# The q and z projections of a decoder layer as seven half-size block products instead of eight, with the head norm of q moved into the attention

## The chip, the cores and the metric

The kernel runs on one core of a Trainium2 chip. The metric is the device time of one execution in microseconds; lower is better. TensorE (PE) multiplies matrices, VectorE (DVE), ScalarE (ACT) and GpSimd (POOL) do the elementwise work, and SyncE (SP) issues every DMA transfer of this kernel from one queue.

## The reference, cut to what matters

Two layers over 2048 tokens of 1024 features, in float32: a gated MLP (layer A), then attention (layer B).

```python
h  = rms_norm(x, norm_g) * (1 + scale) + shift        # layer B; keys and values use an h of their own
qz = h @ w_in                                         # [2048, 1024] @ [1024, 4096]
q  = qz[..., :3072].reshape(2048, 24, 128)            # three groups of eight heads
z  = qz[..., 3072:]
q  = rms_norm(q, q_norm_g) * (128 ** -0.5)            # the head norm, per token and head
# for each group (dilations 1, 4, 16), a band of 128 keys back:
sc = q @ k.T - slope * dilation * distance
p  = exp(sc - max(sc)); l = sum(p); o = p @ v / l
y  = combined(o) * silu(z)
out = x + gate * (y @ w_out)
```

## The kernel before, in words

A TensorE operand here is a pair (hi, lo) whose sum is the float32 number, each part in a shorter format. One product of a k-tile therefore takes three matmuls, hi by hi, hi by lo and lo by hi (`mm3`, lines 241 to 244). Weights are split on the chip, each time they are loaded: ScalarE writes hi and VectorE, or every fourth time GpSimd, writes lo (`split`, lines 219 to 225).

The tokens are worked in four quarters of 512 (four token tiles of 128). In each quarter `layer_A` computes v, u, z and the output product of layer A, and `proj_B` then computes keys and values (`kv_block`, three blocks of 512 columns), q (`q_block`, six blocks) and z of layer B (`z_block`, two blocks). All of these blocks but u and z of layer A go through `dense`: eight k-tiles of weights, 512 columns each, meet two token tiles at a time, so a block is 8 x 4 x 3 = 96 matmuls of 128x512. The weights of a block are loaded 512 KB at a time by `wunits` (line 231) into two buffers (`rp`) and split into nine (`wp`). At the end of `layer_A` the new residual tile is normalised (line 511), transposed on TensorE (line 311), and made into the operands `hk` (for keys and values) and `hb` (for q and z) by `norm_T`.

The result of a q block is normalised per head at once (`head_norm_store`): a square on ScalarE (522), a reduce on VectorE (524), a power on GpSimd (213, 214), a multiplication on VectorE (527), and a store to DRAM (566). Attention later loads it from there in blocks of 128 queries and one key-value head (`attend`), in four stages that run one unit apart: transposes of keys and queries, scores with maximum and exponentials (681 to 685), transposes of the probabilities, and weighted values. VectorE adds the distance times the slope, a constant of the program, to the scores (681).

Attention and the other side work are generators, the fillers. After each k-step of a product, `tick` lets some of their steps be issued; `rate` says how many. The attention of groups 0 and 1 runs beside layer A of the next quarter; group 2 needs all tokens and runs inside the q blocks of quarter 3, at a rate of 5.8 steps a tick; the rest runs in `finish`, which also combines the groups and does the output product. The program is recorded in this order, and a scheduler then orders each engine's instructions and assigns the buffers of the pools before the program is built; on the chip every engine works its own list in order.

Of the kernel before, what the change touches and what calls it, by code (L numbers as in the profile page):

```python
# [18 lines left out]
P = 128  # L19
# [15 lines left out]
def trunk(ctx, tc, out, x, c, a_ada_w, a_ada_b, a_norm_g, a_w_in, a_sgu_g, a_w_spatial,  # L35
# [15 lines left out]
    ep = ctx.enter_context(tc.tile_pool(name="ep", bufs=4))  # L51
    bp = ctx.enter_context(tc.tile_pool(name="bp", bufs=2))
    sp = ctx.enter_context(tc.tile_pool(name="sp", bufs=4))
    ap_ = ctx.enter_context(tc.tile_pool(name="ap", bufs=2))
# [5 lines left out]
    qd = [dp.tile([S, D], F32, name=f"qd{g}") for g in range(3)]  # L60
# [3 lines left out]
    gd = dp.tile([2, D], F32, name="gd")  # L64

    fillers = []

    def fill(n):
        """run n steps of the waiting side work, taking turns"""
# [28 lines left out]
    # ---------------------------------------------------------------- constants  # L98
# [7 lines left out]
    def columns(rows, nm):  # L106
        """vectors (multiples of 128 long) as columns of one tile, with the column of each"""
# [19 lines left out]
    def late_constants():  # L127
# [11 lines left out]
    # distance table for [query i, key j of prev | own]: i - j + 128, BIG outside the band  # L139
    dist = cp.tile([P, 256], F32, name="dist")  # L140
    nc.gpsimd.iota(dist, pattern=[[-1, 256]], base=P, channel_multiplier=1,
                   allow_small_or_imprecise_dtypes=True)
    nc.gpsimd.affine_select(dist, dist, pattern=[[-1, 256]], compare_op=ALU.is_ge,
                            fill=BIG, base=P, channel_multiplier=1)
    nc.gpsimd.affine_select(dist, dist, pattern=[[1, 256]], compare_op=ALU.is_ge,
                            fill=BIG, base=0, channel_multiplier=-1)
# [21 lines left out]
    def column_sums(acc, nm):  # L168
        """sums over the partitions of 512 columns, as four feature-major columns"""
# [17 lines left out]
    def ada_affine(dst, w, bo, go, nm):  # L187
        """dst: (A, B) with h = A * x / rms(x) + B, feature-major columns"""
# [21 lines left out]
    # ---------------------------------------------------------------- helpers  # L210
# [8 lines left out]
    def split(hi, lo, src, pool=False):  # L219
        """src = hi + lo exactly, both in 12 significant bits"""  # L220
# [6 lines left out]
    def wunits(w, k0, n0, nm, nk=KT, ordered=False):  # L227
        us = []
        for kk in range(0, nk, 2):
            raw = rp.tile([P, 2, 512], F32, tag="raw", name=f"raw_{nm}{kk}")  # L230
            ld = nc.sync.dma_start(
                raw, w[(k0 + kk) * P:(k0 + kk + 2) * P, n0:n0 + 512].rearrange("(k p) n -> p k n", p=P))
            if ordered:
                tc.keep_in_program_order(ld)
            for j in range(2):
# [687 lines left out]
```

## Time and profile before

| what | value |
|---|---|
| timed runs before | 3148.74, 3144.09, 3141.40 us; median 3144.09 |
| span of the profiled execution | 3137.5 us |
| median of the timed runs less that span | 6.6 us |
| TensorE busy | 3053.7 us, 97% of the span |
| VectorE, ScalarE, GpSimd busy | 51%, 45%, 32% |
| DMA, mean over the span | 148 GB/s, 463.20 MB |
| granted TensorE clock, mean | 0.991 |

The profile is of one execution. Its own time outside the profiler is not listed; the three timed runs lie 3.9 to 11.2 us above its span, and the span is what the rows add up to. A busy time is the union of the instructions' durations, so overlapping instructions count once. In a row of a group, the number after x is the count, then come the busy time in us, the mean duration of one in ns, and the idle time of the engine just before these instructions with what ended it.

### The profile page before, as it was taken

The numbers are of one execution on the slowest core, as the hardware profiler recorded it, in microseconds if no ns is written. First come the engines' busy times: TensorE is split into PE (matmuls) and PEld (weight loads), VectorE is DVE, ScalarE is ACT, GpSimd is POOL, SyncE is SP. The second block draws the span as 40 slices with busy tenths as digits, with TensorE's granted clock in tenths as the row PEclk, the third lists the DMA queues.
The fourth block names the chain that finished last, engine by engine and source line by source line (L and its number), as shares of the span: only waits on it lengthen the run. The fifth ranks groups of instructions, "written<-read, shape, count | busy, mean of one in ns | idle before, by whom it ended". The sixth has DMA issues, their size and how long they took to land.

```text
span 3137.5 us, 42797 instructions
## 1 busy us (share of the span) xinstructions
PE 3053.7 (97%) x15264; PEld 2562.8 (82%) x15264; DVE 1599.4 (51%) x2808; ACT 1427.5 (45%) x3017; POOL 999.6 (32%) x1080
## 2 busy tenths in 40 slices
PE   6999999999999999999999999999999999999999
PEld 4788878888888878888888888888888778877887
DVE  6785343443544344445654444446554445548853
ACT  4323343346555243356454343465453436566431
POOL 4212233331223133334344233433353231132312
PEclk9999999999999999999999999999999999999999
DMA  6765244443433354443333344433333355567733
GB/s 231 232 205 162 94 147 148 145 158 105 131 108 108 111 158 141 155 149 110 111 105 105 131 146 153 154 125 125 101 100 109 118 174 176 178 209 264 256 131 135
DMA packets 294488, 463.20 MB, mean 148 GB/s; under 512 B 28058, under 2 KB 127612, under 8 KB 294276
## 3 DMA queue, kind: packets, MB, share of 16 engines
q1 hardware_dynamic: 294276, 460.47, 44.9%
q8 instruction: 121, 1.98, 0.3%
q14 instruction: 91, 0.75, 0.1%
HBM read 371.91 MB, written 88.48 MB: 147 GB/s over the span
## 4 chain that ended last, share of the span: by engine, by line
PE 81%; DVE 7%; DMA 5%; issue 3%; POOL 2%; ACT 2%; SPq 1%; POOLq 0%; DVEq 0%; ACTq 0%
PE pd_q L242 5%; PE pd_q L244 5%; PE pd_q L243 5%; PE pd_z L279 4%; PE pd_z L281 4%; PE pd_z L280 4%; PE pd_u L279 3%; PE pd_u L281 3%; PE pd_u L280 3%; PE po L732 3%; PE pd_o L244 3%; PE pd_o L242 3%; PE pd_o L243 3%; PE pd_v L244 3%; PE pd_v L242 3%; PE pd_v L243 3%
## 5 line engine op out<-in xcount | busy, mean ns | idle before, releaser
L242 PE MATMUL pd_q<-w_q,hbh 128*128 128x512 f32 x768 | 305.1, 397 | 0.0
L244 PE MATMUL pd_q<-w_q,hbl 128*128 128x512 f32 x768 | 299.8, 390 | 0.0
L243 PE MATMUL pd_q<-w_q,hbh 128*128 128x512 f32 x768 | 299.4, 390 | 0.0
L685 ACT ACTIVATE pr<-pr,stat 128x256 f32<-128x256 f32 (+1 forms) x384 | 172.7, 451 | 100.0 <-DVE stat L683 99.5
L242 PE MATMUL pd_v<-w_v,hAh 128*128 128x512 f32 x512 | 208.0, 406 | 1.3 <-ACT hAh L322 1.3
L279 PE MATMUL pd_u<-hAh,w_u 128*128 128x512 f32 x512 | 208.5, 407 | 0.0
L279 PE MATMUL pd_z<-hAh,w_z 128*128 128x512 f32 x512 | 204.5, 399 | 0.0
L244 PE MATMUL pd_v<-w_v,hAl 128*128 128x512 f32 x512 | 202.3, 395 | 0.0
L243 PE MATMUL pd_v<-w_v,hAh 128*128 128x512 f32 x512 | 201.9, 394 | 0.0
L281 PE MATMUL pd_u<-hAh,w_u 128*128 128x512 f32 x512 | 200.1, 391 | 0.0
L281 PE MATMUL pd_z<-hAh,w_z 128*128 128x512 f32 x512 | 199.9, 390 | 0.0
L280 PE MATMUL pd_u<-hAl,w_u 128*128 128x512 f32 x512 | 199.8, 390 | 0.0
L242 PE MATMUL pd_o<-w_o,yh 128*128 128x512 f32 x512 | 199.8, 390 | 0.0
L243 PE MATMUL pd_o<-w_o,yh 128*128 128x512 f32 x512 | 199.8, 390 | 0.0
L280 PE MATMUL pd_z<-hAl,w_z 128*128 128x512 f32 x512 | 199.7, 390 | 0.0
L244 PE MATMUL pd_o<-w_o,yl 128*128 128x512 f32 x512 | 199.4, 389 | 0.0
L221 ACT ACTIVATE w_q<-raw_q 128x512 fp32r<-128x512 f32 x192 | 116.2, 628 | 182.9 <-DMA raw_q<-in_b_w_in_dram 122.6
L221 ACT ACTIVATE w_o<-raw_o 128x512 fp32r<-128x512 f32 x128 | 77.9, 628 | 215.0 <-PE pd_o L244 120.5
L244 PEld LDWEIGHTS pd_q<-w_q,hbl 128*128 128x128 f32 x768 | 144.2, 188 | 30.7
L681 DVE SCALAR_TENSOR_TENSOR pr<-dist,ps 128x256 f32<-128x256 f32 (+1 forms) x384 | 118.7, 356 | 98.2 <-PE ps L671 54.5
L242 PEld LDWEIGHTS pd_q<-w_q,hbh 128*128 128x128 f32 x768 | 144.6, 188 | 27.7
L243 PEld LDWEIGHTS pd_q<-w_q,hbh 128*128 128x128 f32 x768 | 144.5, 188 | 27.6
(314 smaller groups left out, 7750.5 us busy)
## 6 DMA issues: line engine op xcount, KB each, us to landing
raw_q<-in_b_w_in_dram SPq DMA_DIRECT2D x96, 512.0 KB, 3.7
raw_v<-in_a_w_in_dram SPq DMA_DIRECT2D x64, 512.0 KB, 3.7
raw_u<-in_a_w_in_dram SPq DMA_DIRECT2D x64, 512.0 KB, 3.9
raw_z<-in_a_w_in_dram SPq DMA_DIRECT2D x64, 512.0 KB, 3.6
raw_o<-in_a_w_out_dram SPq DMA_DIRECT2D x64, 512.0 KB, 3.6
raw_kv<-in_w_kv_dram SPq DMA_DIRECT2D x48, 512.0 KB, 3.8
qd<-hs_q SPq DMA_DIRECT2D x96, 256.0 KB, 2.1
qt<-qd SPq DMA_DIRECT2D x96, 256.0 KB, 2.7
```

What stands on the lines that cost most here:

```text
L221: nc.scalar.activation(hi, src, AF.Copy)
L242: nc.tensor.matmul(pt, lh, u[:, 0, :], start=first, stop=False)
L243: nc.tensor.matmul(pt, lh, u[:, 1, :], start=False, stop=False)
L244: nc.tensor.matmul(pt, ll, u[:, 0, :], start=False, stop=last)
L279: nc.tensor.matmul(pts[i], wh, hh[:, k, :], start=k == 0, stop=False)
L280: nc.tensor.matmul(pts[i], wh, hl[:, k, :], start=False, stop=False)
L281: nc.tensor.matmul(pts[i], wl, hh[:, k, :], start=False, stop=k == KT - 1)
L681: nc.vector.scalar_tensor_tensor(pr[:, i, :], dist[:, 256 - w:256], slope * DIL[g], psc[:, i, :], ALU.mult, ALU.subtract)
L685: nc.scalar.activation(pr[:, i, :], pr[:, i, :], AF.Exp, bias=mneg[:, i:i + 1], scale=-1.0, accum_out=lsum[:, i:i + 1])
L732: nc.tensor.matmul(po[:, h * P:(h + 1) * P], u["pT"][h // hp][:, h % hp, j, :], u["kv"][:, j, kh, 1, :], start=j == 0, stop=j == nk - 1)
```

## The change

q and z of layer B are computed in four blocks of 1024 columns (three groups of q, and z). Each block multiplies [512 tokens x 1024] by [1024 x 1024] as a 2 x 2 arrangement of half-size blocks, by the scheme of Strassen in Winograd's form: seven products of [256 x 512] by [512 x 512] instead of eight, with sums of blocks before and after. In detail:

- The sums of weight blocks (four per block of columns) are computed once, during quarter 0, by a new filler, `combine_weights`, and kept in DRAM (`wt`): t1 and t3 are differences of neighbouring blocks, t2 and t4 differences taken from those.
- The sums of token blocks are made at the end of `layer_A` by `norm_T2`, which takes the place of `norm_T` there: seven operands in place of one `hb`, in four buffers of `big` instead of two.
- `dense_s` runs the seven products, 168 matmuls in all, into two pairs of PSUM tiles in turn, and adds the results on VectorE in new tiles (`st`, pool `tp`).
- The q rows are stored unnormalised, with eight more columns per row: the four head factors, and the slopes divided by them. Attention copies these eight columns (GpSimd), adds the distance times the slope over the factor, takes the maximum, multiplies it by the factor, and lets the exponential scale by the factor.
- Weights are loaded 256 KB at a time into six buffers of half the size, and split into eight instead of nine. The pool of the elementwise tiles (`ep`) has six instead of four. The output weights of `finish` are loaded through the pool `wp`.
- The order in `proj_B` becomes kv 2, kv 1, q 2, kv 0, q 1, q 0, z. The rates change: 1.7 instead of 1.5 in quarter 0 (which has the weight sums as well), 0.7 instead of 1.3 for the next quarter's input, 7.0 instead of 5.8 for group 2.

```diff
-    wp = ctx.enter_context(tc.tile_pool(name="wp", bufs=9))
-    rp = ctx.enter_context(tc.tile_pool(name="rp", bufs=2))
+    wp = ctx.enter_context(tc.tile_pool(name="wp", bufs=8))
+    rp = ctx.enter_context(tc.tile_pool(name="rp", bufs=6))
...
+    def combine_weights():
+        for b in range(4):
+            for k in range(4):
...
+                nc.vector.tensor_tensor(t1, q[0, 1], t1, ALU.subtract)
+                nc.gpsimd.tensor_tensor(t3, q[1, 1], t3, ALU.subtract)
+                yield
+                nc.vector.tensor_tensor(t2, t2, t1, ALU.subtract)
+                nc.gpsimd.tensor_tensor(t4, t4, t2, ALU.subtract)
+                for i, t in enumerate((t1, t2, t3, t4)):
+                    nc.sync.dma_start(wt[b][i][k * P:(k + 1) * P, :], t)
...
+        def product(pts, a, w, first):
+            us = wunits(*src[w], f"{nm}{w}_", 4)
+            hh, hl = ops[a]
+            for k in range(4):
+                for i in range(2):
+                    sl = slice(i * P, (i + 1) * P)
+                    mm3(pts[i], hh[:, k, sl], hl[:, k, sl], us[k], first and k == 0, k == 3, True)
+                tick(0.2857)
...
+        product(x, "11", "11", True)
+        u2 = tmp("u")
+        for i in range(2):
+            nc.scalar.activation(u2[i][:, 0:512], x[i], AF.Copy)
+        product(y, "s2", "t2", True)
+        add(u2, y, u2)
+        product(x, "12", "21", False)
+        for i in range(2):
+            evac(i, x[i], 0)
+        product(y, "s3", "t3", True)
+        u3 = tmp("v")
+        add(u3, y, u2)
+        product(x, "s1", "t1", True)
+        add(u3, x, u3)
+        for i in range(2):
+            evac(i + 2, u3[i], 1)
+        product(y, "22", "t4", False)
+        c21 = tmp("w")
+        add(c21, y, u2)
+        for i in range(2):
+            evac(i + 2, c21[i], 0)
+        product(x, "s4", "22", False)
+        add(u2, x, u2)
+        for i in range(2):
+            evac(i, u2[i], 1)
...
-                slope = 2.0 ** (-8.0 * (g * 8 + kh * 4 + h + 1) / NH)
-                nc.vector.scalar_tensor_tensor(pr[:, i, :], dist[:, 256 - w:256], slope * DIL[g],
-                                               psc[:, i, :], ALU.mult, ALU.subtract)
-            nc.vector.tensor_reduce(mneg, pr, AX.X, ALU.min)
+                nc.vector.scalar_tensor_tensor(pr[:, i, :], dist[:, 256 - w:256], u["rt"][:, h:h + 1],
+                                               psc[:, i, :], ALU.mult, ALU.add)
+            mx = u["rt"][:, 8 + c * hp:8 + (c + 1) * hp]
+            nc.vector.tensor_reduce(mx, pr, AX.X, ALU.max)
+            nc.vector.scalar_tensor_tensor(mneg, mx, -1.0, u["rt"][:, 4 + c * hp:4 + (c + 1) * hp],
+                                           ALU.mult, ALU.mult)
```

More of the change, by code (lines that the diff above doesn't have):

```diff
@@ L59, in trunk @@
     kvd = dp.tile([S, 3, 512], F32, name="kvd")
[L60 removed]
+    qd = [dp.tile([S, 2, 520], F32, name=f"qd{g}") for g in range(3)]
     od = [dp.tile([S, D], F32, name=f"od{g}") for g in range(3)]
@@ L64, in trunk @@
     gd = dp.tile([2, D], F32, name="gd")
+    wt = [[dp.tile([512, 512], F32, name=f"wt{b}_{i}") for i in range(4)] for b in range(4)]
     fillers = []
@@ L495, in layer_A @@
         hk = (bigr(f"hkh{Q}"), bigr(f"hkl{Q}"))
-        hb = (bigr(f"hbh{Q}"), bigr(f"hbl{Q}"))
+        hb, keep = new_ops(f"b{Q}"), {}
         for n in range(2):
@@ L580, in proj_B @@
+        for f, n in ((kv_block, 2), (kv_block, 1), (q_block, 2), (kv_block, 0), (q_block, 1),
+                     *(((ahead, None), (q_block, 0)) if Q + 1 < NQ else ((q_block, 0), (ahead, None))),
+                     (z_block, 0)):
             if f is kv_block and n == 0 and Q == NQ - 1:
                 fillers.append(attend([(2, b) for b in range(16)]))
-                rate[0] = 5.8
+                rate[0] = 7.0
             f(n)
```

185 lines of the change are left out of this document (142 added, 43 removed).

## Prediction

> **What bounds the kernel now.** I read the page first: busy shares and the granted clock.
>
> ```profile
> span 3137.5 us, 42797 instructions
> PE 3053.7 (97%) x15264; PEld 2562.8 (82%) x15264; DVE 1599.4 (51%) x2808; ACT 1427.5 (45%) x3017; POOL 999.6 (32%) x1080
> ...
> PEclk9999999999999999999999999999999999999999
> ```
>
> PE is busy for 97% of the span at full clock; no other engine is over 51%. Next, the waits of PE, longest in total first, to see whether that share hides stalls:
>
> ```profile
> PE pc_a L412 <- DVE acc_a L408: 23.5, 4, 17.4
> PE pt_b L311 <- DVE xr L511: 14.9, 8, 4.0
> PE pf L858 <- DVE yb L848: 8.7, 4, 3.4
> PE pp L720 <- ACT pr L685: 5.9, 5, 3.2
> ```
>
> The largest is the start-up, once; the next is the turn from layer A to layer B, four times; the list falls off at once. So a matmul taken away is time taken away, unless something else becomes late. For the price of a matmul its own duration will not do, because matmuls overlap; the timeline of PE inside a q block gives the spacing:
>
> ```profile
> 500.07 0.39 PE L243 MATMUL pd_q<-w_q,hbh 128*128 128x512 f32 x1
> ...
> 509.82 0.39 PE L244 MATMUL pd_q<-w_q,hbl 128*128 128x512 f32 x1
> ```
>
> Between these two starts lie 43 steps of the gap-free stream: 9.75 / 43 = 0.2267 us each, not the 0.39 of a row.
>
> **Term 1, the matmuls removed.** Counts by group, and the windows of the stages that the other terms use (columns: window, length, busy of PE, PEld, DVE, ACT, POOL, clock, DMA share, GB/s):
>
> ```profile
> L242 PE MATMUL pd_q<-w_q,hbh 128*128 128x512 f32 x768 | 305.1, 397 | 0.0
> L242 PE MATMUL pd_z00b<-w_z00b,hbh 128*128 128x512 f32 x32 | 12.7, 396 | 0.0
> 118.00:250.00 132.00, 128.37 (x614) 105.53 (x613) 100.85 (x156) 39.48 (x73) 18.92 (x19) 1.00 0.64 205
> 250.00:340.00 90.00, 90.00 (x395) 72.65 (x394) 42.42 (x58) 36.41 (x61) 21.61 (x17) 1.00 0.41 135
> 340.00:429.00 89.00, 88.83 (x400) 73.47 (x399) 33.51 (x50) 26.19 (x51) 22.85 (x20) 1.00 0.35 114
> 429.00:481.00 52.00, 47.92 (x207) 39.37 (x206) 27.43 (x41) 27.41 (x56) 20.67 (x20) 0.93 0.50 160
> ...
> 547.00:634.00 87.00, 87.00 (x385) 72.09 (x384) 36.86 (x57) 28.01 (x48) 31.22 (x40) 1.00 0.45 151
> ...
> 2575.00:2616.00 41.00, 37.32 (x225) 31.20 (x224) 21.75 (x50) 23.86 (x67) 8.35 (x11) 1.00 0.53 173
> 2618.00:2774.00 156.00, 155.04 (x951) 133.42 (x951) 87.54 (x199) 92.61 (x282) 28.89 (x40) 1.00 0.55 179
> 2775.00:2815.00 40.00, 35.19 (x180) 28.50 (x179) 14.14 (x31) 25.30 (x54) 21.06 (x13) 0.91 0.72 216
> 2815.00:2855.00 40.00, 38.07 (x227) 31.87 (x225) 29.77 (x74) 31.99 (x77) 5.46 (x4) 1.00 0.66 233
> 2855.00:2955.00 100.00, 90.41 (x531) 78.67 (x532) 88.44 (x210) 51.59 (x154) 32.49 (x17) 0.95 0.81 280
> ```
>
> Three lines issue q: 3 x 768 = 2304 matmuls, and each of eight z blocks has 3 x 32 = 96, together 3072. A new block (1024 columns) is 7 products x 4 k x 2 token tiles x 3 = 168; sixteen of them make 2688. The instruction order of the built program shows the same numbers. So 384 go, 384 x 0.2267 = 87.1 us. No matmul is added: sums of inputs, of weights and of products run on VectorE, ScalarE and GpSimd. More than 87.1 could only come out of PE's old waits, and the largest of them, the start-up, is not touched; I count no gain there. The other terms are what fails of the cover: work that moves to engines which are not the bound costs nothing as long as PE never has to wait for it.
>
> **Term 2, the new blocks themselves** (quarters 0 to 2, twelve blocks). PE needs 168 x 0.2267 = 38.1 us for one. The rows of the pieces:
>
> ```profile
> L221 ACT ACTIVATE w_q<-raw_q 128x512 fp32r<-128x512 f32 x192 | 116.2, 628 | 182.9 <-DMA raw_q<-in_b_w_in_dram 122.6 <-PE pd_q L244 41.8 <-PE pd_kv L244 13.8
> L225 DVE TENSOR_TENSOR w_q<-raw_q,w_q 128x512 fp32r<-128x512 f32 x144 | 96.2, 690 | 120.9 <-ACT w_q L221 120.8
> L225 POOL TENSOR_TENSOR w_q<-raw_q,w_q 128x512 fp32r<-128x512 f32 x48 | 68.4, 1426 | 198.5 <-ACT w_q L221 198.5
> L225 DVE TENSOR_TENSOR w_kv<-raw_kv,w_kv 128x512 fp32r<-128x512 f32 x72 | 63.9, 905 | 73.8 <-ACT w_kv L221 73.1
> L522 ACT ACTIVATE hs_q<-pd_q 128x512 f32<-128x512 f32 x96 | 54.4, 590 | 117.8 <-PE pd_q L244 115.4
> L524 DVE TENSOR_REDUCE s_q<-hs_q 128x4 f32<-128x512 f32 x96 | 63.4, 683 | 97.0 <-ACT hs_q L522 97.0
> L503 DVE TENSOR_TENSOR xo<-pd_o,ga 128x512 f32<-128x512 f32 x32 | 21.2, 685 | 58.6 <-PE pd_o L244 58.6
> L213 POOL TENSOR_SCALAR hr_q<-s_q 128x4 f32<-128x4 f32 x96 | 18.5, 193 | 196.5 <-DVE s_q L524 190.9
> L214 POOL TENSOR_TENSOR hr_q<-hr_q,mhalf 128x4 f32<-128x4 f32 x96 | 96.7, 1008 | 8.0
> L231 SPq DMA_DIRECT2D raw_q<-in_b_w_in_dram x96: 367/373/1320, 463.6 to 2723.6; - x96
> ```
>
> ScalarE: 28 splits x 0.628 + 12 copies and squares x 0.590 = 24.7 us. VectorE: 21 x 0.690 + 10 sums from PSUM x 0.685 + 8 reduces x 0.683 = 26.8; with the worst mean, 0.905, 31.4. GpSimd: 7 x 1.426 + 8 x (0.193 + 1.008 + two small operations between 0.193 and 1.008) = 22.7 to 35.7; I take the low end, since those two are plain products without the power. SyncE: 28 loads and 8 stores x 0.373 = 13.4. DMA: 28 x 262 KB + 8 x 266 KB = 9.5 MB, 248 GB/s, where the q stage (547 to 634) had 151; between it and the 280 of the last row. So nobody passes 38.1 us. Cover in time: the eight weight tiles are two products deep (one feeds 6 matmuls, 1.36 us), so a freed tile is due again 7 x 1.36 = 9.5 us later, and loading and splitting it takes about a load's issue, its flight and 0.628 + 0.690. Each pair of PSUM tiles rests for one other product, 24 x 0.2267 = 5.4 us, against two sums of 0.685 that empty it. Queued behind a sum on VectorE are the next product's weight splits, and PE waits for both. Before, tiles had about the same lead, but a split fell due every 2.7 us; now every 1.36. In return VectorE loses the 96 multiplications of the old head norm (line 527), since the factors now go with the stored rows. Bounds: zero, or the share PE lost where VectorE was at 88% and DMA at 280 GB/s (9.6 of 100 us in the last row): 3.7 us a block, 44 in all. The 70% load is nearer to the q stage, which lost nothing: I take 0.8 a block, **10 us**.
>
> **Term 3, quarter 3,** where attention of group 2 runs inside these blocks, 7 steps a tick instead of 5.8.
>
> ```profile
> L685 ACT ACTIVATE pr<-pr,stat 128x128 f32<-128x128 f32 x113 | 43.8, 390 | 22.6 <-DVE stat L683 22.6
> ...
> L221 ACT ACTIVATE w_q<-raw_q 128x512 fp32r<-128x512 f32 x32 | 20.0, 628 | 22.0 <-PE pd_q L244 11.7 <-DMA raw_q<-in_b_w_in_dram 5.9 <-PE pd_kv L244 4.0
> L522 ACT ACTIVATE hs_q<-pd_q 128x512 f32<-128x512 f32 x16 | 9.2, 592 | 4.5 <-PE pd_q L244 3.7
> ...
> L645 PE MATMUL pq<-ident,qt 128*128 128x128 f32 x92 | 13.8, 273 | 0.0
> ```
>
> From 2575 to 2774 ScalarE was busy 23.86 + 92.61 us, less 20.0 + 9.2 for splits and squares, over 113 / 4 = 28 units: at most 3.1 us a unit. PE: 92 / 4 = 23 units cost 156 - 87 = 69 us, 3.0 each. A new block takes 14 units: PE 38.1 + 42 = 80, ScalarE 24.7 + 43.4 = 68, 85% where it had 59%. VectorE gains one tiny product a chunk (max times factor) in front of the exponentials and GpSimd one copy of eight columns a unit; the four stages of attention run one unit apart, and that skew covers both in every quarter. Bounds 0 to 9.6% of the 165 us of two blocks, 16; I take **7**. Behind it, the output weights now pass through the tiles of the product weights, and their second half waits for operands that z still reads: eight issues on SyncE that stand before z's second weights, and PE waits. The old stall there was 4.8 + 1.9 us (two rows from 2775); I take **4** more, bounds 0 to 15.
>
> **Term 4, the turn to layer B,** four times:
>
> ```profile
> 443.18 0.75 DVE L511 TENSOR_SCALAR xr<-xr,r_b 128x1024 f32<-128x1024 f32 x1 [2.46 <-DMA x1d<-xr]
> 444.08 3.96 PE L311 MATMUL pt_b<-ident,xr 128*128 128x128 f32 x16 [4.03 <-DVE xr L511]
> ```
>
> VectorE had 2.46 us idle in front of this, which hides what the first token pair adds. For the second pair each half of the features now brings four sums and two or three more splits, and in the built order most of them stand between the feature groups that kv needs: 0 to 6 x 0.905 = 5.4 us. Kv itself spends 12 x 0.2267 = 2.7 us on a group of two k, so about half stays hidden; I take 3 each: **12**. The wait also cools the clock: 0.93 in that window. The Trainium skill (TensorE: Matmul & The Clock Gate, "What's actually happening") halves the clock after an idle window of about 3.4 us; the window's 0.93 agrees, and by that rule a longer wait would cost some 2 us more each time, 8 in all, and the sum below would be 41.
>
> **Term 5, quarter 0.** Weight sums: 64 loads and 64 stores of 262 KB, 33.6 MB, beside u, z and the first output half. Those ran at 0.64, 0.41 and 0.35 DMA share, so idle DMA there is 132 x 0.36 + 90 x 0.59 + 45 x 0.65 = 130 us; 205 GB/s at 0.64 is 320 at full share, and 33.6 MB need 105. It fits, tightly early on: 0 to 20, I take **4**. SyncE's 128 issues of 0.373 are 48 us of 311. Start-up (slopes on an idle GpSimd, loads cut in two): **1**.
>
> **Sum.** 87.1 - 10 - 7 - 4 - 12 - 4 - 1 = 49 us. The profiled span goes from 3137.5 to about 3088.5; the timed median lies 6.6 above that span, which I keep: 3144.1 - 49 = 3095.
>
> **Rivals.** *Cover holds everywhere*: 87 less the 3 or so of start-up and quarter 3, 3060. For it: in the windows of 156 us from 2618 and of 87 us from 547 PE lost at most 1 us, with VectorE at 56% and 42%. Against: splits come twice as fast, and the loads here are 65 to 85%. Chance 0.18. *DMA late in quarter 0 and in the blocks*: stores that wait for VectorE and GpSimd hold SyncE's queue, and the product weights stand behind them. With terms 2 and 5 at their upper ends (44 for 10, 20 for 4) 50 us more are lost and nothing is gained, 3145; with half of that 24 us are left, 3120. For it: 248 GB/s asked of each block. Against: six loads ahead and two products of split tiles. Chance 0.15, of which 0.11 stays faster, 0.03 within 0.2%, 0.01 slower. *VectorE becomes the bound, slower*: its splits read two SBUF tensors and meet GpSimd's longer list.
>
> ```profile
> L225 DVE TENSOR_TENSOR w_v<-raw_v,w_v x90: 669/693/1784, 62.2 to 2124.9; 128x512 fp32r<-128x512 f32 x90
> ```
>
> If every split took that maximum, a block would need 21 x 1.784 + 12.4 = 49.9 us, 11.8 over PE: 16 x 11.8 = 189, net 102 slower, 3246. It decides from a mean split of about 1.40 us (16 x 3.7 eats the 59 us that the other terms leave). Worst mean before: 0.905. Chance 0.09. The Trainium skill (SBUF — State Buffer, "Who interferes with whom") says that a VectorE instruction with two SBUF inputs waits out a GpSimd one that reads SBUF; the 1784 against 669 agrees, and the sums from PSUM would be free of it. *The change does not do what it says* is excluded by the count of matmuls.
>
> **Numbers.** Forecast 0.58, rivals 0.18, 0.15, 0.09 in the order above. About 0.2% (6.3 us) is what a measurement can tell from no change. Faster 0.58 + 0.18 + 0.11 = 0.87, same 0.03, slower 0.09 + 0.01 = 0.10. Range: from full cover (3144 - 87 = 3057) past the halved second rival to 3130, which leaves out the worst third of that rival and the third one, with a little below 3057: under 2 in 10.
>
> **What would show it.** Right: spacing 0.2267 in the new products, 38 to 39 us a block in quarters 0 to 2, PE waits on weight splits or sums of under 1 us a block. Wrong: blocks of over 42 us; mean split on VectorE over 1.4 us; waits of PE on DMA between 118 and 429; window clock under 0.95 inside the blocks; q blocks of quarter 3 over 90 us.

## The result, and the profile after

The kernel after takes 3180.52 us (median; 3177.94 to 3188.67), the kernel before, timed beside it, 3146.41. The ratio is 1.0119, 95% interval 1.0101 to 1.0138: slower by 1.2%, where 1.6% faster was forecast. The profiled execution took 3181.95 us with a span of 3180.2, 42.7 more than the span before.

The page of the kernel after, span and busy line:

```profile
span 3180.2 us, 45171 instructions
...
PE 3009.1 (95%) x14880; PEld 2501.6 (79%) x14880; DVE 1905.3 (60%) x3258; ACT 1622.4 (51%) x3288; POOL 1212.6 (38%) x1468
```

15264 - 14880 = 384 matmuls are gone, as counted, and TensorE's busy time fell from 3053.7 to 3009.1. The span grew all the same, so PE now waits where it didn't. Its waits, longest in total first (total us, times, longest):

```profile
PE pc_a L556 <- DVE acc_a L552: 21.8, 4, 16.8
PE pd_o L247 <- POOL w_o L231: 17.4, 5, 9.3
PE pq L803 <- DMA qt<-qd: 11.4, 4, 8.3
PE pd_kv L247 <- ACT hkh L444: 10.6, 8, 2.4
PE pf L1022 <- DVE yb L1012: 9.8, 5, 3.6
PE pc_ksc L177 <- DVE acc_ksc L169: 7.5, 2, 7.1
PE pyb L1009 <- POOL og L1004: 7.4, 1, 7.4
PE pd_q10a L247 <- DVE w_q L231: 6.0, 1, 6.0
PE pd_q00a L247 <- DVE w_q L231: 6.0, 1, 6.0
```

The start-up still leads, and the wait for `yb` in the last stage (L1022) is near its old size (8.7 us before). The other rows are waits that before did not have, or had smaller: the output weights of layer A on GpSimd (none before), the attention's queries on a DMA (1.4 us), the operands of keys and values on ScalarE (none), the column sums of the affines on VectorE (3.6), the first y of the last stage on GpSimd (none), and once in each of quarters 0 to 2 the weights of q of group 0 (none; the third, 5.4 us, is just below these rows). Where the block products have nothing else beside them they run without a gap, as the timeline of PE shows for q of group 2 in quarter 0 (one row is one product of 24 matmuls):

```profile
534.53 5.60 PE L247 MATMUL pd_q02a<-w_q,hob 128*128 128x512 f32 x24
539.97 5.60 PE L247 MATMUL pd_q02b<-w_q02t,hob 128*128 128x512 f32 x24
```

5.44 / 24 = 0.2267 us, and 38.08 us for the block. The loss is elsewhere. The windows of after (same columns as before: window, length, PE, PEld, DVE, ACT, POOL, clock, DMA share, GB/s), first u, z and the output product of quarter 0, then q of group 1, q of group 0 and z, then q of group 0 and z of quarter 3:

```profile
141.00:272.00 131.00, 115.20 (x528) 91.35 (x528) 108.25 (x161) 32.35 (x56) 33.27 (x25) 0.93 0.84 272
272.00:370.00 98.00, 91.10 (x389) 72.75 (x388) 48.45 (x52) 30.95 (x55) 43.13 (x29) 0.98 0.77 249
370.00:481.00 111.00, 94.37 (x401) 75.64 (x400) 43.22 (x60) 31.24 (x59) 34.58 (x28) 0.94 0.47 154
...
594.00:632.00 38.00, 38.00 (x170) 31.46 (x169) 25.62 (x38) 22.94 (x39) 20.40 (x27) 1.00 0.64 202
632.00:681.00 49.00, 43.02 (x184) 34.95 (x183) 35.12 (x55) 29.80 (x59) 30.92 (x51) 0.93 0.60 197
681.00:723.00 42.00, 40.21 (x187) 33.05 (x186) 32.72 (x41) 23.41 (x41) 27.96 (x31) 1.00 0.79 265
...
2737.00:2817.00 80.00, 76.09 (x476) 63.33 (x475) 54.39 (x122) 62.47 (x168) 31.99 (x54) 1.00 0.77 254
2818.00:2900.00 82.00, 72.15 (x399) 59.80 (x398) 60.26 (x116) 58.25 (x120) 31.13 (x35) 0.94 0.65 205
```

PE's busy column is short of the window's length in every window but q of group 1, and the clock falls below 1.00 in five of them. Taking each stage from the start of its first product to the start of the next stage's in the timelines of both kernels (the last stage up to the end of its last product, 5 us before the span's end), the account closes:

| stage | before | after | against what the change should give |
|---|---|---|---|
| layer A, quarter 0 (v, u, z, output) | 401.1 | 453.8 | 52.7 lost |
| output product and first two kv blocks, quarters 1 and 2 | 141.7, 140.8 | 146.5, 146.5 | 5 lost each, 16 over the turns |
| q of groups 2 and 1, each | 43.52 | 38.08 | 5.44 gained, nothing lost |
| q of group 0 and z, quarters 0 to 2 | 90.9, 90.9, 91.6 | 91.0, 95.0, 89.9 | 35 lost (10.9 a quarter should go) |
| quarter 3 from kv block 0 to the end | 557.6 | 571.2 | 30 lost (16.3 should go) |

Layer A of quarters 1 to 3 is 3.2 shorter. 52.7 + 15.7 + 35.2 + 29.9 - 3.2 = 130.3 lost and 87.1 gained make 43.2, where the span grew by 42.7. The prediction had 38 for the same losses.

### The profile page after: what moved, and what is told of

Same layout as the page of the kernel before. It is cut to its first block, busy times and chain, and to the rows that moved or that the text cites. A ratio compares the mean times of both kernels' runs of the same rounds, so it can differ in the third digit from the quotient of the medians.

```text
span 3180.2 us, 45171 instructions
## 1 busy us (share of the span) xinstructions
PE 3009.1 (95%) x14880; PEld 2501.6 (79%) x14880; DVE 1905.3 (60%) x3258; ACT 1622.4 (51%) x3288; POOL 1212.6 (38%) x1468
## 5 line engine op out<-in xcount | busy, mean ns | idle before, releaser
L247 PE MATMUL pd_v<-w_v,hAh 128*128 128x512 f32 x1024 | 328.2, 402 | 1.2 <-ACT hAh L405 1.2
L247 PE MATMUL pd_kv<-w_kv,hkh 128*128 128x512 f32 x768 | 245.3, 400 | 11.4 <-ACT hkh L444 10.6
L247 PEld LDWEIGHTS pd_o<-w_o,yh 128*128 128x128 f32 x1024 | 195.3, 191 | 68.6 <-POOL w_o L231 19.8
L849 ACT ACTIVATE pr<-pr,stat,rt 128x256 f32<-128x256 f32 (+1 forms) x384 | 208.1, 543 | 47.3 <-DVE stat L845 46.3
L247 PEld LDWEIGHTS pd_v<-w_v,hAh 128*128 128x128 f32 x1024 | 190.6, 192 | 40.7 <-issue 2.7
L841 DVE SCALAR_TENSOR_TENSOR pr<-dist,rt,ps 128x256 f32<-128x256 f32 (+1 forms) x384 | 142.3, 416 | 108.3 <-PE ps L832 45.8
L247 PEld LDWEIGHTS pd_kv<-w_kv,hkh 128*128 128x128 f32 x768 | 145.9, 192 | 47.2 <-ACT hkh L444 14.0
L896 PEld LDWEIGHTS po<-kv,pT 128*128 128x128 f32 x1200 | 147.0, 191 | 15.6 <-ACT pT L765 5.3
L247 PE MATMUL pd_kv<-w_kv,hkl 128*128 128x512 f32 x384 | 153.4, 403 | 3.0 <-DVE hkl L445 3.0
L896 PE MATMUL po<-kv,pT 128*128 128x128 f32 x1200 | 152.1, 277 | 2.1 <-ACT pT L765 1.1
```

The lines of the kernel that those rows point to most:

```text
L247: nc.tensor.matmul(pt, a, u[:, w, :], start=f, stop=e, skip_group_check=more)
L841: nc.vector.scalar_tensor_tensor(pr[:, i, :], dist[:, 256 - w:256], u["rt"][:, h:h + 1], psc[:, i, :], ALU.mult, ALU.add)
L849: nc.scalar.activation(pr[:, i, :], pr[:, i, :], AF.Exp, bias=mneg[:, i:i + 1], scale=u["rt"][:, h:h + 1], accum_out=lsum[:, i:i + 1])
L896: nc.tensor.matmul(po[:, h * P:(h + 1) * P], u["pT"][h // hp][:, h % hp, j, :], u["kv"][:, j, kh, 1, :], start=j == 0, stop=j == nk - 1)
```

## Experiments

Each ratio is to the kernel before, timed beside it. "Q0" is layer A of quarter 0, "tail" the three blocks q of group 1, q of group 0 and z summed over quarters 0 to 2 (353.4 of it for nine blocks of 38.08 and the transposes of the next input), "Q3" is quarter 3 from its first kv block to the end. All are us of the profiled execution. The Q3 column needs care. In seven of the kernels below the edit leaves quarter 3 alone (no sums, sums moved only, on VectorE and spread, input beside z alone, normalisation split and pinned), and still Q3 lies between 657 and 677 us. Each profile is of one execution, and the timed runs of one kernel spread by up to 17 us (three edits together: 3128.96 to 3146.09). A difference of less than 20 us in that column proves nothing by itself.

| kernel | median | ratio, 95% interval | Q0 | tail | Q3 |
|---|---|---|---|---|---|
| before | 3146.41 | 1 | 401.1 | 403.9 | 652.6 |
| after | 3180.52 | 1.0119 [1.0101, 1.0138] | 453.8 | 390.2 | 662.7 |
| eight products | 3146.97 | 1.0007 [0.9997, 1.0016] | 406.4 | 404.2 | 660.9 |
| no sums | 3139.59 | 0.9981 [0.9971, 0.9990] | 408.2 | 393.7 | 664.1 |
| sums moved only | 3136.98 | 0.9970 [0.9957, 0.9983] | 405.9 | 388.2 | 668.2 |
| sums on VectorE | 3154.18 | 1.0025 [1.0016, 1.0035] | 431.4 | 386.0 | 661.0 |
| sums spread | 3146.59 | 0.9996 [0.9986, 1.0007] | 419.9 | 390.3 | 661.9 |
| input beside z alone | 3182.13 | 1.0116 [1.0101, 1.0131] | 454.8 | 391.7 | 657.1 |
| normalisation split | 3199.67 | 1.0176 [1.0160, 1.0191] | 450.8 | 394.1 | 676.7 |
| normalisation pinned | 3191.57 | 1.0138 [1.0112, 1.0164] | 451.4 | 385.7 | 673.4 |
| factors on VectorE | 3205.05 | 1.0188 [1.0171, 1.0205] | 454.4 | 390.9 | 680.1 |
| rate 5.8 | 3184.09 | 1.0123 [1.0108, 1.0138] | 451.1 | 392.5 | 661.2 |
| q of group 2 earlier | 3181.15 | 1.0102 [1.0083, 1.0122] | 453.7 | 394.7 | 658.3 |
| three edits together | 3137.06 | 0.9971 [0.9960, 0.9983] | 418.0 | 378.2 | 652.3 |
| ... with sums at 2.9 steps | 3162.86 | 1.0047 [1.0030, 1.0065] | 443.6 | 381.1 | 661.0 |
| ... with 1.5 steps beside z | 3140.13 | 0.9984 [0.9972, 0.9996] | 421.3 | 378.1 | 655.3 |
| ... with both and thin input | 3139.33 | 0.9987 [0.9975, 0.9999] | 442.2 | 366.9 | 662.0 |
| ... with thin input | 3129.71 | 0.9949 [0.9934, 0.9964] | 421.5 | 363.7 | 669.7 |
| ... with thin input and fraction 0.0 | 3122.66 | 0.9928 [0.9903, 0.9953] | 420.4 | 363.4 | 657.4 |
| ... with thin input and fraction 0.5 | 3123.48 | 0.9934 [0.9913, 0.9954] | 419.0 | 362.9 | 661.0 |

**Which half of the change costs: eight products.** The block products undone, the head norm in the attention kept.

```diff
-            dense_s(hb, g, f"q{Q}{g}", ev)
+            for n in range(2):
+                dense([hb], b_w_in, g * D + n * 512, f"q{Q}{g}{n}", lambda t, pt, n=n: ev(t, pt, n))
```

> One part alone: eight products as before (no weight sums, no sums of inputs, operands of b as two buffers, the old order with the next input before z and the old rates), while the rest of the change stays (q stored unnormalised with its factors, the factors applied in the attention, loads of 512 columns by one k, the same pools). Theory A (the seven-product scheme with its sums causes the loss; the head norm part is about neutral): 3140 to 3155, that is near the kernel before. Rival F (the head norm inside the attention and the longer chain to the stored query cost 20 us or more of the loss, in kv of group 0 and in quarter 3): 3165 to 3185.

1.0007: theory A; the head norm half makes no difference that the timing can tell. The turn to layer B is back at 141.8 us (146.5 after), so the 5 us there are those of `norm_T2`. In quarter 3 this kernel's profile still has 8 us more than before's, all of them in z (87.9 us for 79.8). It keeps the head norm in the attention and the output weights' new buffers; whether one of these is the cause or only the scatter of Q3 was not tried.

**Quarter 0: no sums, and sums moved only.** The first leaves `combine_weights` out; the second keeps its 128 transfers and drops the four differences:

```diff
-                nc.vector.tensor_tensor(t1, q[0, 1], t1, ALU.subtract)
-                nc.gpsimd.tensor_tensor(t3, q[1, 1], t3, ALU.subtract)
                 yield
-                nc.vector.tensor_tensor(t2, t2, t1, ALU.subtract)
-                nc.gpsimd.tensor_tensor(t4, t4, t2, ALU.subtract)
```

> The sums of weights in quarter 0 are left out (no loads, differences or stores of them); the four products that used them read raw quadrants of the same weight, so the matmuls and loads of layer B stay in number and size and only the values differ. Theory A (three quarters of the lost time is spread over three places; quarter 0 pays about 52 us for the sums): about 3128 us, 52 below the changed kernel, with u, z and the output block of quarter 0 back at about 110, 89 and 89 us, and q0 blocks, turns and quarter 3 as slow as in the changed kernel. Rival B (the whole loss is in the seven-product blocks and quarter 0 only absorbs time that is lost anyway, or the clock): within 15 us of the changed kernel. Rival C (stores of the sums also slow what follows): under 3115.

> The loads and the stores of the weight sums stay, the four differences are left out (the quadrants are stored as they are). Theory A (the price in quarter 0 is the order on the engines' queues: GpSimd stands waiting in a difference for its load, and the work of z and of the output weights queues behind it): gains 30 to 50 of the 52 us, about 3135 to 3150. Rival B (33.6 MB of transfers beside u: DMA share 0.84 in that stage, so the loads of the u weights come late): gains under 15 us, above 3165, and u stays at about 130 us.

Without the sums 1.4% of the time is gone: 41 us between the medians, 46 in quarter 0 of the profiles, where theory A expected 52. With the transfers but without the differences just as much is gone (44 and 48). Two windows of the latter, u and z of quarter 0:

```profile
141.00:256.00 115.00, 112.03 (x537) 91.28 (x536) 92.75 (x146) 32.25 (x56) 13.78 (x13) 0.99 0.93 313
256.00:345.00 89.00, 89.00 (x392) 72.70 (x391) 30.95 (x43) 38.09 (x64) 23.59 (x17) 1.00 0.97 317
```

The DMA engines are at 0.93 and 0.97 of their time, above the 0.84 of after, and PE loses 3 us in u and nothing in z. Bandwidth is not the price. What is, the queues of after show. From the waits of GpSimd and of VectorE over the whole kernel, those for the sums (the first row is the attention's copy of the factors, which comes up under quarter 3):

```profile
POOL rt L813 <- DMA qt<-qd: 227.5, 56, 13.0
...
POOL st_cw L303 <- DMA st_cw<-in_b_w_in_dram: 74.9, 9, 18.0
```

```profile
DVE st_cw L302 <- DMA st_cw<-in_b_w_in_dram: 41.5, 11, 8.6
DVE st_cw L305 <- POOL st_cw L303: 41.2, 14, 7.3
```

And the timeline of GpSimd early in the output product:

```profile
383.08 1.26 POOL L303 TENSOR_TENSOR st_cw<-st_cw,st_cw 128x512 f32<-128x512 f32 x1 [5.97 <-DMA st_cw<-in_b_w_in_dram]
385.15 1.67 POOL L306 TENSOR_TENSOR st_cw<-st_cw,st_cw 128x512 f32<-128x512 f32 x1 [0.81 <-DVE st_cw L305]
386.78 11.64 POOL L630 TENSOR_TENSOR yl<-mt,yh 128x512 fp32r<-128x512 f32 x8
398.39 1.25 POOL L231 TENSOR_TENSOR w_o<-raw_o,w_o 128x512 fp32r<-128x512 f32 x1
```

GpSimd stands 5.97 us in front of a difference whose load has not landed, then does a second one; eight subtractions for y (L630) have queued up behind them and take 11.64 us, and the split of an output weight stands behind those, for which PE waits 9.3. ScalarE had finished its part of that weight by 381.4 us, 17 us before GpSimd came to it. GpSimd works its list in order, so one instruction that waits for a DMA holds all that stands behind it.

About as much as in the output product (22 of the 52.7 us) was lost in u (20); z lost 9 and v 2. In the window of u PE is idle for 15.8 us, and 13.8 of them are waits for the column sums of the affines. Their accumulations run on VectorE among the differences. VectorE is 83% busy in that window and stands 13.5 us in front of differences, 7.6 for loads and 5.9 for GpSimd. This trace does not separate that standing from the work of the differences; the next edits do so in part.

**Sums on VectorE, spread, sooner.** All four differences on VectorE; then also pinned in program order two steps behind their loads, beside the affines' sums at 2.4 steps a tick; then, on the three edits together, at 2.9.

```diff
-                nc.gpsimd.tensor_tensor(t3, q[1, 1], t3, ALU.subtract)
+                keep(nc.vector.tensor_tensor(t3, q[1, 1], t3, ALU.subtract))
...
-    fillers.append(side_work())
-    rate[0] = 1.7
+    fillers.append(rest_of_ada())
+    fillers.append(combine_weights())
+    rate[0] = 2.4
```

> All four differences of the weight sums on VectorE, nothing on GpSimd; all else as in the changed kernel. Theory A (GpSimd's queue): z and the output block of quarter 0 lose their 8.6 and 21.9 us, u gets no better or a little worse, since VectorE takes 32 differences more of about 0.7 us: 3150 to 3165. Rival B (transfers): no change, 3175 to 3185. Rival D (VectorE's own queue, waiting for the same loads, is the bound): slower than 3185.

> The weight sums stay whole, but all differences are on VectorE, pinned in program order two steps behind their loads, and they run side by side with the gates' and affines' sums at 2.4 steps a tick, from the first v block on, so that nothing is left to be run at once ahead of the second output block. Theory A (quarter 0 pays for queues, not for transfers or for work): u, z and the output block of quarter 0 return to within 5 us of 112, 88 and 93 (as without the sums); 30 to 45 us below the changed kernel, 3135 to 3150. Rival G (VectorE's extra 64 differences of about 0.7 us are 45 us of work that u has no room for): 3150 to 3165, with u over 118.

> The three edits together, and the weight sums and gates of quarter 0 at 2.9 steps a tick in place of 2.4, so that the sums end inside z and not at its turn to the output block, where PE waited 8.9 us; nothing else. Theory A (the wait is the last differences, standing for their loads on VectorE ahead of the multiplications that the output block needs): the output block of quarter 0 falls from 99 to 90 to 93 us, u and v grow by at most 3: 3130 to 3134. Rival L (the sums take the time wherever they stand): no change in the sum over v, u, z and the output block, 418 us, 3135 to 3140.

On VectorE z returns to 88.4 us, and u, which was expected to gain nothing, falls to 120.9. The output block stays at 107.4, since what is left of the sums is issued at once ahead of its second half. Spread, u is 109.9 with all 64 differences on VectorE: there was room for the work. v pays 3 and the output block still 8 us. This edit changes the engine, the order, the distance to the load and the rate at once; which of these counts most was not tried. At 2.9 (3162.86 us) the output block is at 92.9 as expected, but v, u and z are at 125, 122 and 103 us, where they were at 118, 109 and 91, and the kernel is 26 us slower than at 2.4, not 3 to 7 faster. The waits of that kernel between 125 and 480 us, ScalarE's and the DMA queue's:

```profile
ACT w_u L227 <- DMA raw_u<-in_a_w_in_dram: 69.5, 24, 10.4
...
ACT w_z L227 <- DMA raw_z<-in_a_w_in_dram: 54.1, 21, 7.3
```

```profile
SPq L309 <- DVE st_cw L303: 58.4, 12, 9.0
```

The stores of sums (L309 there) hold SyncE until VectorE has done the differences, and loads of weights stand behind them. At 2.4, in the three edits together, the same three waits are 66.2, 24.1 and 37.1 us. So the weights of z came later at 2.9, and that fits what z lost. The weights of u were waited for about as long at 2.4, where u lost nothing; what v and u pay at 2.9 is open. With the same transfers and no differences u and z lost 3 us, though SyncE stood 42.7 us in front of stores whose loads had not landed.

**Q of group 0 and z.** Four edits. The next input beside z alone; its normalisation in separate steps; these pinned in VectorE's order; and, on the three edits together, the input over three blocks:

```diff
+        with tc.issue_after(red.ins):
+            for t in range(TPQ):
+                tc.keep_in_program_order(
+                    nc.vector.tensor_scalar(xts[t], xts[t], rs[t][:, 0:1], None, ALU.mult))
...
-                     *(((ahead, None), (q_block, 0)) if Q + 1 < NQ else ((q_block, 0), (ahead, None))),
+                     *(((ahead, None), (q_block, 1), (q_block, 0)) if Q + 1 < NQ else
+                       ((q_block, 1), (q_block, 0), (ahead, None))),
```

> The next quarter's input is made beside z alone (after q of group 0) at 1.3 steps a tick, where the changed kernel makes it beside q of group 0 and z at 0.7. Theory A (33 us of quarters 0 to 2 are lost because its normalisation, a chain between GpSimd and VectorE, stands ahead of the weight splits of q of group 0): q of group 0 falls to 38 us each and z takes part of it back: 3155 to 3170. Rival B (the loss belongs to the seven-product block as such and to the load of VectorE, wherever the input is made): same total, 3175 to 3190.

> The next quarter's input is normalised in separate steps: first the squares, reduces and powers of all four token tiles, and in later steps the four scalings; 0.75 steps a tick for the one step more. Theory A (VectorE stands 11 us in a ping-pong with GpSimd's powers, and product sums and weight splits queue behind it): q of group 0 falls from 48.5 to 40 to 43 us in quarters 0 to 2 and 15 to 25 us are saved in all, 3156 to 3166. Rival B (GpSimd's and VectorE's load in these blocks, not the order, is the price): under 6 us saved, 3174 to 3184.

> As the split normalisation, but VectorE's order is pinned: the four reduces stand together, two weight splits behind them, then the four scalings, each behind what was issued before it; so the powers on GpSimd run while VectorE has other work (the split without pins left the reduces and scalings in alternation in the issued order). Theory A (VectorE's 11 us ping-pong is what q of group 0 and z lose): VectorE's idle time in front of the scalings falls from about 7 to about 2 us a quarter, q of group 0 from 48.5 to 42 to 45 us in quarters 0 to 2, z no longer than 43; 10 to 20 us in all, 3160 to 3170. Rival B (the load of the engines, not the order): q of group 0 stays at 48 or z grows by what q loses.

> The three edits together, and the next quarter's input is spread over three blocks (q of group 1, q of group 0, z) at 0.48 steps a tick in place of two at 0.75; nothing else. With nothing lost the three blocks would take 3 x 38.08 and 3.6 us of transposes, 117.8 us; in the three edits together they took 125.4, 125.5 and 127.3. Theory A' (what is left there is load: VectorE at 72 and 82% in those blocks, with splits of 1.09 us beside a busy GpSimd, 67% in the blocks without the input; a thinner input lets PE catch up): 119 to 122 us each, 10 to 18 us in all, 3119 to 3127. Rival J (each step of the input costs PE the same wherever it stands): 125 to 128 each, 3134 to 3140.

Beside z alone, q of group 0 is at 38.4 to 39.1 us and z takes back all of it (52 to 55), as rival B has it: the place doesn't matter. The split did not do what it meant to: in the issued order the reduces and scalings stood in alternation again, and VectorE's wait was unchanged (6.8 us in quarter 0); it tests nothing there. This is that place in the timeline of VectorE of after:

```profile
643.35 0.75 DVE L474 TENSOR_SCALAR x<-x,r_a 128x1024 f32<-128x1024 f32 x1 [3.96 <-POOL r_a L220]
...
645.13 0.75 DVE L474 TENSOR_SCALAR x<-x,r_a 128x1024 f32<-128x1024 f32 x1 [0.96 <-POOL r_a L220]
...
648.65 1.74 DVE L474 TENSOR_SCALAR x<-x,r_a 128x1024 f32<-128x1024 f32 x1 [0.94 <-POOL r_a L220]
650.32 1.28 DVE L231 TENSOR_TENSOR w_q<-raw_q,w_q 128x512 fp32r<-128x512 f32 x2
```

From 639.4 to 650.3 VectorE does 4.4 us of work, because each scaling waits for a power on GpSimd and the next reduce stands behind it; the weight split that PE needs comes at 650.32. Pinned, that wait is gone and q of group 0 is at 42.9 to 44.2 us, but z gives two thirds of it back: the tail falls by 4.5 us, not 10 to 20 (by 12 with the sums spread as well). So this order is a third of the 35 us at most. Both edits took more time in all, 19 and 11 us, most of it in quarter 3 (14 and 11 us in the profiles), which they leave alone; that is within the scatter of Q3. The windows of q of group 0 and z with the three edits, and of q of group 1, q of group 0 and z with the thin input:

```profile
595.00:639.00 44.00, 41.12 (x182) 32.87 (x182) 31.34 (x49) 27.26 (x56) 29.04 (x46) 1.00 0.69 219
639.00:683.00 44.00, 41.73 (x193) 33.39 (x192) 36.23 (x51) 26.49 (x48) 30.82 (x38) 1.00 0.79 254
```

```profile
556.00:595.00 39.00, 39.00 (x175) 32.29 (x175) 26.59 (x43) 25.23 (x52) 20.03 (x27) 1.00 0.69 216
595.00:634.00 39.00, 39.00 (x179) 32.27 (x179) 32.16 (x44) 22.98 (x42) 29.29 (x42) 1.00 0.68 222
634.00:678.00 44.00, 40.88 (x185) 32.37 (x184) 35.68 (x47) 25.20 (x44) 29.27 (x38) 1.00 0.80 268
```

With eight products the input ran beside z, and cost nothing, at this load:

```profile
633.00:681.00 48.00, 48.00 (x226) 39.66 (x226) 22.31 (x38) 24.91 (x50) 20.60 (x28) 1.00 0.51 167
```

VectorE was at 46% there and is at 71 and 82% beside the seven products. Thinned out, the three blocks take 122.4, 120.3 and 121.1 us, theory A' to within 0.4, and two of them run without a gap; the 10 us left over the three quarters lie in z. VectorE's share alone does not decide, though: q of group 0 loses nothing at 82%, z loses 3 us at 81%. Shown is that fewer steps of the input beside each product let PE catch up; why z still doesn't is open.

**Quarter 3.** The factors' copy on VectorE, the old rate, q of group 2 ahead of kv block 1, and, on the three edits together, 1.5 steps a tick beside z:

```diff
-        nc.gpsimd.tensor_copy(rt[:, 0:8], u["qt"][:, 512:520])
+        nc.vector.tensor_copy(rt[:, 0:8], u["qt"][:, 512:520])
...
-                rate[0] = 7.0
+                rate[0] = 5.8
...
-        for f, n in ((kv_block, 2), (kv_block, 1), (q_block, 2), (kv_block, 0), (q_block, 1),
+        for f, n in ((kv_block, 2),
+                     *(((kv_block, 1), (q_block, 2)) if Q + 1 < NQ else ((q_block, 2), (kv_block, 1))),
+                     (kv_block, 0), (q_block, 1),
```

> The attention's copy of the eight factors of a query tile (128x8) is made on VectorE, not on GpSimd; all else as in the changed kernel. Theory A for quarter 3 (GpSimd's queue stands in that copy until the query's load lands, 227 us of waiting in the trace, and weight splits and factors of q stand behind it): q1, q0 and z of quarter 3 get 8 to 15 us shorter, about 3167 to 3173. Rival B (that wait is harmless, or VectorE now stands in it instead): 3176 to 3186, or slower than that, up to 3195, where VectorE waits for the load.

> In quarter 3 group 2's attention is released at 5.8 steps a tick instead of 7.0, so that its last steps come out in front of z instead of inside q of group 0. Theory A (the blocks of quarter 3 lose PE time because too many attention steps stand between the products): 3 to 8 us shorter than the changed kernel, 3173 to 3178. Rival B (the lost 30 us come from the query load at the start, the table switches and GpSimd in z, and the start of the last stage; the rate is not in it): within 3 us, 3178 to 3184. Rival E (the steps left over then run with nothing beside them): 3185 to 3195.

> In quarter 3 alone q of group 2 is made ahead of kv block 1, so that the rows that group 2's attention loads are stored a kv block (21.8 us) earlier. Theory A (8.3 us of PE's wait at the start of kv block 0 come from the longer chain to the stored q: sum, square, reduce, four GpSimd operations, store, load): kv block 0 falls from 50.6 to about 43 us, 3172 to 3176. Rival H (the keys of kv block 1, stored just before, are late too, or the wait moves on to the next query): 3177 to 3184.

> The three edits together, and 1.5 steps a tick of the last attention beside z of quarter 3 in place of 3.0, so 12 of its steps run in the last stage as in the kernel before; nothing else. Theory A' (z of quarter 3 loses because the attention, the output weights' splits and z's own sums share VectorE and GpSimd in it): z falls from 96 by more than the last stage gains, 4 to 10 us net, 3127 to 3133. Rival K (the steps cost the same in either place): z falls by 13 to 16 and the last stage grows by as much, 3134 to 3140.

The copy on VectorE costs 25 us more, outside what either theory allowed. The 227.5 us that GpSimd stands in it over the whole kernel (L813, above) looked like a culprit; on VectorE the wait is shorter,

```profile
DVE rt L813 <- DMA qt<-qd: 108.9, 46, 9.7
```

but Q3 grows by 17 us. That the sums of the scores and the weight splits, which stand in VectorE's queue behind the copy, cause this is likely and not shown, since Q3 scatters as widely without any edit to it. What is shown is that the wait on GpSimd was not worth moving; whether it costs anything there is open. The rate is not the cause (rival B). With q of group 2 earlier, kv blocks 1 and 0 together fall by 8.3 us, just the wait of pq; but z grew by 6.3 and the ratio's interval overlaps that of after (rival H). Fewer steps beside z (3140.13 us) only move: z 14.5 us shorter, the last stage 17 longer (rival K).

**Together, and the fraction of a step.** The pinned normalisation, the spread sums and the earlier q of group 2:

> The three edits together (pinned normalisation, spread sums on VectorE, q of group 2 earlier in quarter 3). If the three causes are separate and each theory holds: 3110 to 3130, faster than the kernel before by 0.5 to 1%. If only the sums count: 3135 to 3150, about the kernel before. If the engines' load is the bound, what one place gains the next loses: over 3150.

> All of these together: three edits, thin input, 1.5 steps in z of quarter 3, sums at 2.9. If the gains are separate and theory A' holds: 3105 to 3118. If each gives back elsewhere what it gains: 3130 to 3140.

> The three edits together with the thin input, and the fraction of a step that tick carries along is set to 0.0 where group 2's attention begins; not one instruction is added or taken away. Theory M (in quarter 3 the exact places of the attention's steps between the products, a matter of that fraction, move its time by 10 us and more: 652 to 680 us in kernels whose edits are elsewhere): this run and the one at 0.5 differ by 6 us or more, or both stand 6 us or more off the thin input's 3130. Rival N (the 17 us more that quarter 3 took in the thin-input kernel come from the thin input itself, or from the run): both at 3126 to 3133, with quarter 3 from its first kv block to the end at 667 to 672 us.

> The same with the fraction set to 0.5. Theory M: 6 us or more off the run at 0.0 or off 3130. Rival N: 3126 to 3133.

The three together give 3137 us, 0.3% under the kernel before and 7 over the expectation for three separate causes: the sums give 36 us of profile, the tail 12, and Q3 10, which is within its scatter. With the thin input, 2.9 steps and 1.5 beside z it is 3139.33, where 2.9 takes back what the rest gains. The thin input alone takes 14.4 us off the tail, but 7 off the time, 2.7 less than theory A' allowed; Q3, which it leaves alone, is 17 us longer in that profile. Setting the carried fraction where group 2 begins, and nothing else, brings Q3 from 669.7 to 657.4 and 661.0 us and the time to 3122.66, 0.7% under the kernel before (0.5 to 1.0%). That is what theory M expected. But each Q3 is of one execution (at 0.0 the fastest of four, which lie between 3116.01 and 3131.68), and the intervals of the timed ratios overlap that of the thin input. So how much the fraction moves the time is not settled.

## Why the prediction was wrong

**The gain (term 1)** held to the matmul: 384 gone, 0.2267 us apart, 38.08 us a block.

**Term 5, quarter 0**, is the step that failed most: 4 us, bounds 0 to 20, measured 52.7. It asked whether 33.6 MB fit into the idle time of the DMA engines, and they do (0.97 and nothing lost). It priced no difference: 32 on GpSimd and 32 on VectorE, each able to stand in its queue until a load lands. The bound belonged to the engines' queues. With the transfers alone quarter 0 takes 405.9 us, and with all differences on VectorE, well behind their loads, 419.9. Without the sums 408.2 remain, 7 over before, 4 of them in the output product.

**Term 2** put 10 us on twelve blocks. Six of them, q of groups 2 and 1, lost nothing, and the range of 0 to 44 holds the 35 that the other six lost. But these are q of group 0 and z, where the next quarter's input runs, and the term costed blocks without it. The sign shown there (blocks over 42 us, clock under 0.95) came: 48.9 us and 0.93. The timeline of PE prices the clock as well:

```profile
651.05 6.87 PE L247 MATMUL pd_q00a<-w_q,hob 128*128 128x512 f32 x17 [5.98 <-DVE w_q L231]
657.76 1.55 PE L247 MATMUL pd_q00b<-w_q00t,hob 128*128 128x512 f32 x6
```

After the wait of 5.98 us, 17 matmuls took 6.71 us, not 17 x 0.2267 = 3.85: 2.9 more. The window of these rows has a granted clock of 0.77:

```profile
649.00:664.00 15.00, 12.95 (x47) 10.43 (x48) 12.95 (x19) 7.78 (x14) 6.51 (x9) 0.77 0.60 188
```

The Trainium skill (TensorE: Matmul & The Clock Gate, "What's actually happening") has the clock halve after such a wait; these rows agree. The prediction drew about 2 us a time from it, for the turns to layer B; here it is 2.9, in a place for which it was not asked.

**Term 3** said 11, measured 30 (23 to 44 in the seven kernels that leave quarter 3 alone). Set against what the change should give, kv block 0 takes 7 us too much, q of groups 1 and 0 take 20, z takes 16, and the last stage takes 13 less. Of the waits, 8.3 us are the first wait for a query, behind the longer chain to the stored q, for which the prediction had no term. The factors are not what makes it long: the eight-product kernel stores the same rows and waits 2.9 there (before: 1.4). Most of it comes with the seven products; that it is because their last results come at the end of the block is read from the program, not tested. PE's waits for z's weights, where the prediction put 4, are 3.6. 7.4 us are the first y of the last stage behind its chain on VectorE and GpSimd. The rest is scattered over q of groups 1 and 0 and z, and stays open.

**Term 4**, 12 for the turns, measured 16, and eight products show that `norm_T2` is its cause. The 8 us that a colder clock was to add there did not come: no wait of PE on the operands (L444) is longer than 2.4 us, and the clock of the turn is 0.97 where it was 0.93.

**The rivals.** The first, cover everywhere, held in six of the twelve blocks. The second named stores that hold SyncE's queue; in the kernel after SyncE waited 30.1 us for differences of VectorE and 26.5 for GpSimd's between 125 and 480 us. But ScalarE waited only 11.3 us for the weights of u there, 34.5 before, so this was not the price; at 2.9 steps a tick it is part of what z lost, if that reading holds. The third, VectorE through slower splits, came half way: beside z the splits took 1.17 to 1.24 us where eight products had 0.69 to 0.91, below its point of 1.40. The real mechanism, an engine that waits in order for a load with urgent work queued behind, was none of the rivals, although the prediction asked what stands behind a sum on VectorE inside the blocks. It did not ask it in quarter 0.

## What to carry to other kernels

Work moved off the bound engine is free only where it doesn't wait in front of something urgent on its new engine, and mean shares of busy time don't show that. So cost it by place: list, for each added instruction, what it waits for, what stands behind it, and which side work runs beside it. And put an operation that waits for a load two or more steps behind that load, pinned if a scheduler may move it; the spread sums did so, among other changes.

## What the runs showed of the hardware that was not expected

DMA engines at 0.97 of their time, 317 GB/s, did not slow weight loads enough for PE to lose anything (z of quarter 0, sums moved only). A wait of 5.98 us cost PE 8.8 us, with the slow products after it.

The splits of z's weights on VectorE, in z of eight products with GpSimd at 43% and in z of after with GpSimd at 67%:

```profile
L231 DVE TENSOR_TENSOR w_z00b<-raw_z00b,w_z00b 128x512 fp32r<-128x512 f32 x3 | 2.1, 693 | 3.8 <-ACT w_z00b L227 3.8
...
L231 DVE TENSOR_TENSOR w_z0b<-raw_z0b,w_z0b 128x512 fp32r<-128x512 f32 x6 | 7.3, 1237 | 1.3 <-ACT w_z0b L227 1.3
L341 DVE TENSOR_TENSOR st_z0bv<-pd_z0bb,st_z0bv 128x512 f32<-128x512 f32 x2 | 1.4, 680 | 0.0
```

The same split of 128x512 took 0.69 to 0.91 us in the one and 1.17 to 1.24 in the other, while the sums that read one of their operands from PSUM (the last row) stayed at 0.68 beside the busy GpSimd. And in quarter 3 the same instructions in another interleaving, by a fraction of a step, took 657 to 670 us, in one profiled execution each.
